# Output projections: the split of a row hung behind a product, one row ahead instead of two; the second pair's Gram masks 18 products sooner

## The chip, the core and the metric

The kernel runs on one core of a Trainium2 chip. The metric is the device time in microseconds (us) of one execution, as the median of several runs. The engines are called as the profile calls them: PE (TensorE, matrix products), DVE (VectorE), ACT (ScalarE), POOL (GpSimd) and SP (SyncE, which here issues most of the DMA transfers).

## What is computed

Two residual layers over 512 tokens of width 2048, in float32. Layer 0 is a gated differential attention with 8 heads, layer 1 a gated RWKV-7 time mixing with 32 heads of 64 channels; each ends with an output projection and a residual add. Cut to what matters:

```
for i in range(2):
    hn = rms_norm(x, norm_w[i])
    if i == 0:
        q, k, v, gate = split(hn @ w_in)            # 2048 -> 4 * 2048
        a = softmax(q1 k1^T) - lam * softmax(q2 k2^T)   # causal, per head
        y = rms_norm(a v) * silu(gate)
        out = y @ w_out                             # 2048 -> 2048
    else:
        p = hn @ w_in                               # 2048 -> 4 * 2048 + 2 * 96
        p = p + (shift(p) - p) * mu
        r, k, v, g, dw, da = split(p)
        for t in range(512):                        # per head, state S is 64 x 64
            S = S * w_t + (S a_t) b_t^T + v_t k_t^T
            y_t = S r_t
        out = (group_norm(y) * silu(g)) @ w_out     # 2048 -> 2048
    x = x + out
```

## The kernel before

Everything is computed with 128 partitions. A product in float32 precision is made of three products of halves: each operand is split into a rounded high half (hH, wh) and the rest (hL, wl), and `mm3` (line 118) issues high*high, high*low and low*high. A split is always one cast on ACT and one subtraction on DVE: lines 109 and 110 for weights (wh, wl from wraw), lines 474 and 475 for rows of activations (hH, hL from yr).

**Input projections** (`unit_chan`) give one block of 128 channels by 512 tokens in a bank pp: 16 blocks of the contracted dimension, three products each, so 48 products. Its argument `behind` is a list of pairs (number of products, function): when the count of products is reached, the function is called with the last product as `m` and issues its work there.

**Layer 1** handles two heads, a pair of 64 channels each, at a time: pair j has its own r, k, v and gate blocks. In `receptances(j)` the r block of pair j is projected, and work of pair j-1 hangs on its products: `mask_gram` masks the Gram products of pair j-1 with four affine selects on POOL (lines 1412 and 1414, two for each head). The hook stands at 45 for j = 1 and 2 and at 27 from j = 3 on. "Second pair" below is the pair masked in `receptances(2)`. Around it stand the scan's small products: gp (line 1367, the Gram product of AR with BK), sm (lines 1587, 1600, 1609), px (lines 1494 and 1509, the triangular solve), and ACT's copies of their results: rhs (line 1590), VS (1602), X (1497). AR (line 1351) is made on DVE of the shifted mix mixr (lines 1177 and 1178 hold the shift's two steps; mixE is the same for the gate). sHx (line 1145) is a cast for another product of the pair.

**Output projections** are made by `unit_tok`, 512 columns at a time: outputs are tokens by columns, in four banks, and weights come in steps of two rows of blocks (KG = 2), so 24 products for a step. Its callback `more` is called ahead of the triple products 0, 2 and 4 of a step with a row number n and the last product m. In the first column block of each layer the callback `all_rows` calls the object `feed` of class `Feed`, which loads the rows y of the mixer's output from DRAM (yd, yd2) and splits them with `split_row`. Its constructor loads six rows and splits four; then each call with n splits up to row n + 2 and loads up to row n + 8. In layer 0 some of these rows lie in a buffer Tt, the others in yr. The attention of the last head (exponentials p, lines 407 and 415; transposes pt, line 421) and in layer 1 the scan of the last pairs run among the products of that column block.

Two means set the order. `tc.issue_after(ins)` makes what is issued within it follow an instruction in a scheduler's list. `behind(g, ins, m)` gives one instruction an edge behind product m that orders it in its queue. Both only set the order of the queues: the instruction doesn't wait on the chip for the product.

Of the kernel before, what the change touches and what calls it, by code (L numbers as in the profile page):

```python
# [13 lines left out]
F32 = mybir.dt.float32  # L14
# [369 lines left out]
def attention(g, h, qkT, qkL, sq, vg, gap, rows=None, yT=None):  # L384
# [81 lines left out]
    if yT is not None:  # L466
        rows += [split_row(g, yT[:, c, :]) for c in range(2)]


def split_row(g, yr):  # L470
    nc = g.nc
    hh = g.hp.tile([P, T], F32R, name="hH", tag="hH")
    hl = g.hp.tile([P, T], F32R, name="hL", tag="hL")
    nc.scalar.copy(hh[:], yr)
    g.rowsplit = nc.vector.tensor_sub(hl[:], yr, hh[:].bitcast(F32)).ins
    return hh, hl


class Feed:
# [10 lines left out]
            self.raw.append(self.home(k))  # L490
            self.g.nc.sync.dma_start(out=self.raw[k], in_=self.src[k * P : (k + 1) * P, :])

    def split(self, upto, after=None):
        for k in range(len(self.rows), min(upto, self.n)):
            with self.g.tc.issue_after(after) if after else ExitStack():
                self.rows.append(split_row(self.g, self.raw[k]))

    def __call__(self, n):
        self.split(n + 2, self.g.split)
        self.load(n + 8)  # L500


# [25 lines left out]
class Seven:  # L528
# [70 lines left out]
    def behind(self, raw, h, i):  # L599

        if h + 1 < NH:
            landed = self.g.nc.gpsimd.tensor_copy(self.mark[:], raw[:, 0, 0:1])
            with self.g.tc.issue_after(landed.ins):
                self.prime(h + 1, True, GROUPS[i : i + 1])
        return raw
# [256 lines left out]
def layer0(g, aps):  # L862
    nc, tc = g.nc, g.tc
# [86 lines left out]
    with ExitStack() as cx:  # L950
# [15 lines left out]
        for h in range(1, NH):  # L966
# [3 lines left out]
        feed = Feed(g, g.yd, KT - 2, lambda k: g.work.tile([P, T], F32, name="yr", tag="t1", bufs=4)[:] if k & 4 else  # L970
                    Tt[:, k % 4])
        rows = feed.rows
        ch = Chain(g, attention(g, NH - 1, *before, 22, rows, Tt[:, 4:6]), 12)

        def all_rows(n, _):
            feed(n)
            if n >= KT - 1:
                ch.finish(g)

# [114 lines left out]
        def products(k, wt, s, m):  # L1094
            for c in range(2):
                wh, wl = [x[:, k % 4, c * RK : (c + 1) * RK] for x in wt]
                m = mm3(nc, pts[c][:RK, s], wh, wl, g.hH[k][:, s], g.hL[k][:, s],
                        k == 0 and s.start == 0, k == KT - 1, g, True)
            return m


        m, wts = g.m, []
        turns = [(k, half) for half in range(2) for k in range(0, KT // 2, 2)]
        for i, (k, half) in enumerate(turns):
# [6 lines left out]
            for kk in (k, k + 1):  # L1111
                m = products(kk, wts[kk // 4], slice(256 * half, 256 * half + 256), m)
        for k in range(KT // 2, KT):
# [3 lines left out]
            m = products(k, wts[k // 4], slice(0, T), m)  # L1117
        g.dwda = []
        for i in range(2):
            m = shift_mix(g, pts[i], RK, g.mut[:, i : i + 1], g.omut[:, i : i + 1], "t1", 4)  # L1120
# [51 lines left out]
@urgent  # L1172
def shift_mix(g, ps, rows, mu, omu, tag, bufs=2):

    nc, w = g.nc, g.work
    o_ = w.tile([P, T], F32, name="mix" + tag, tag=tag, bufs=bufs) if tag else g.ys.pop(0)
    nc.scalar.activation(o_[:rows, :], ps[:rows, :], AF.Copy, scale=omu)
    nc.vector.scalar_tensor_tensor(o_[:rows, 1:], ps[:rows, 0 : T - 1], mu, o_[:rows, 1:], ALU.mult, ALU.add)
    return o_
# [84 lines left out]
def mus(g, i, j):  # L1264
    n = i * 16 + j
    return g.mu[:, n : n + 1], g.omu[:, n : n + 1]
# [90 lines left out]
def gram(g, j, p):  # L1357

    nc, w, BK = g.nc, g.work, p.BK
    p.G = w.tile([P, NC_, 2, 2, C], F32, name="G1", tag="G1", bufs=2)  # L1360
    halves = []
    for c0, tag in ((0, "pb"), (4, "pc")):
        gp = [g.ps.tile([P, 512], F32, name="gp", tag=tag, bufs=2) for _ in range(2)]
        halves.append((c0, gp))
        for i in range(4):
            for h, r_ in ((0, slice(0, C)), (1, slice(C, P))):
                m = nc.tensor.matmul(gp[h][:, i * P : (i + 1) * P], BK[r_, c0 + i, :, :], p.AR[r_, c0 + i, :, :],  # L1367
                                     start=True, stop=True)
    p.LP = w.tile([P, NC_, HALF], F32, name="LP", tag="tmpl", bufs=1)
    with g.tc.high_priority(offset=AHEAD):  # L1370
        for c0, gp in halves:
            for h in range(2):
                for half in range(2):
                    q, o = h * C + half * HALF, half * HALF
                    nc.scalar.copy(p.LP[q : q + HALF, c0 : c0 + 4],
                                   gp[h][q : q + HALF].rearrange("p (u x) -> p u x", u=4)[:, :, o : o + HALF])

    def grams(c0, gp):
        for h in range(2):
            nc.scalar.copy(p.G[:, c0 : c0 + 4, :, h, :], gp[h][:].rearrange("p (u x t) -> p u x t", u=4, x=2))  # L1380

    g.soon.append(lambda: grams(*halves[0]))
    g.late.append(lambda: grams(*halves[1]))
    if not j:
        soon(g)
        soon(g, g.late)


def norms(g, j, p, m):

    nc, w = g.nc, g.work
    while g.later:
        g.later.pop(0)()
    ps = g.ps.tile([P, 512], F32, name="pt", tag="pb", bufs=2)
    with g.tc.issue_after(m.ins):
        sum_channels(g, ps[:2, :], g.ones[:, 0 : P : C], p.k2)
    ss = w.tile([2, T], F32, name="ssl", tag="thg", bufs=1)
    nc.scalar.copy(ss[:].rearrange("h (b c t) -> h c b t", b=2, c=NC_), ps[:2, :].rearrange("h (c b t) -> h c b t", c=NC_, b=2))
    nd = g.nd[j % 2]
    for half in range(2):  # L1400
        x = ss[:, half * NC_ * HALF : (half + 1) * NC_ * HALF]
        nc.gpsimd.dma_start(out=nd[:, half].rearrange("h r c t -> h r (c t)"),
                            in_=x[:, None].to_broadcast([2, NG, NC_ * HALF]))
    p.n2 = g.small.tile([P, HALF], F32, name="n2", tag="n2", bufs=1)
    nc.gpsimd.dma_start(out=p.n2[:], in_=nd.rearrange("h b r c t -> (h b r c) t"))


def mask_gram(g, p, h, m=None):

    nc = g.nc  # L1410
    for r_ in [slice(h * C, h * C + C)]:
        a = nc.gpsimd.affine_select(out=p.G[r_, :, 0, 1 - h, :], in_=p.G[r_, :, 0, 1 - h, :], compare_op=ALU.is_ge,
                                fill=0.0, base=-1, pattern=[[0, NC_], [1, C]], channel_multiplier=-1)
        b = nc.gpsimd.affine_select(out=p.G[r_, :, 1], in_=p.G[r_, :, 1], compare_op=ALU.is_ge, fill=0.0, base=0,
                                pattern=[[0, NC_], [0, 2], [1, C]], channel_multiplier=-1)
        behind(g, a, m)
        behind(g, b, m)
# [265 lines left out]
def layer1(g, aps):  # L1683
    nc, tc = g.nc, g.tc
    with ExitStack() as cx:
# [5 lines left out]
        pairs = []  # L1691

        def proj(i, j, **k):
            return unit_chan(g, aps["rw_w_in"][i, j], P, **k)[0]
# [10 lines left out]
        def receptances(j):  # L1705
            def piece(f, i, p):
                def follow(m):
                    with tc.high_priority(offset=SCAN), tc.issue_after(m.ins):
                        f(g, i, p)
                return follow  # L1710

            behind = [(39 if j == 1 else 39, lambda m: norms(g, j, pairs[j], m))]
            if j:
                behind += [(27 if j > 2 else 45, lambda m: [mask_gram(g, pairs[j - 1], h, m) for h in range(2)]),
                           (18 if j == 1 else 12, piece(t_first, j - 1, pairs[j - 1])),
                           (39 if j == 1 else 33, piece(t_second, j - 1, pairs[j - 1]))]
            return shift_mix(g, proj(0, j, behind=behind), P, *mus(g, 0, j), "r", 1)
# [3 lines left out]
        for j in range(D // P):  # L1721
# [16 lines left out]
            def behind(m, j=j, p=p):  # L1738
                if j > 1:
                    pairs[j - 2].chain.finish(g)  # L1740
                with tc.issue_after(m.ins):
                    gram(g, j, p)
                p.solve = Solve(g, t_solve(g, j, p))
# [23 lines left out]
        feed = Feed(g, g.yd2, KT - 2, lambda k: w.tile([P, T], F32, name="yr", bufs=1, tag=(  # L1767
            "r", "k", "th0", "th1", "l", "f", "xH", "xL")[k % 8])[:])
        rows = feed.rows

        def all_rows(n, m):
            feed(n)
            q = pairs[j - 1]
            if n >= 6 and not q.done:
                q.chain.finish(g)
                with tc.issue_after(m.ins):
                    finish_y(g, j - 1, q)
                    gated(g, j - 1, q, gts[0], True)
            if n >= 8 and len(rows) == KT - 2:
                rows.append(split_row(g, gts[0][:]))  # L1780
            if n >= KT and len(rows) < KT:
                p.chain.finish(g)
                finish_y(g, j, p)
                gated(g, j, p, gts[1], True)
                rows.append(split_row(g, gts[1][:]))
# [31 lines left out]
        for nm in ("11", "21", "22", "12"):  # L1817
            t, c = PLACES[nm]
            a = g.low.tile([P, 2, 512], F32, name="acc", tag="AR", bufs=3)
# [76 lines left out]
```

## Time and profile before

| | us |
|---|---|
| median of 3 runs | 2085.77 |
| lowest, highest run | 2085.66, 2087.77 |
| the profiled execution's own time | 2087.6 |
| its span in the profile | 2085.9 |
| PE busy in the span | 2066.0 |
| DVE, ACT, POOL busy | 1655.5, 1255.4, 392.3 |

The span is what the hardware profiler saw between the first and the last instruction of one execution; 1.7 us lie around it. In the profile's rows a time counts from the span's start, "L118" is line 118 of the kernel, and what stands in brackets is the idle time of the engine ahead of that instruction and what ended it. The granted clock (PEclk) is the share of its full rate that TensorE's clock was allowed, 1.00 at most. The layer 0 output projection starts at about 740 us, the Gram of the second pair lies near 1080 us, and layer 1's output projection starts at about 1895 us.

### The profile page before, as it was taken

How to read it: one execution, taken by the hardware profiler on the slowest of the kernel's cores; microseconds unless marked ns; L12 is line 12 of the kernel's file. 1: busy time of each engine (PE TensorE's matmuls, PEld its weight loads, DVE VectorE, ACT ScalarE, POOL GpSimd, SP SyncE). 2: the span in 40 equal slices, each digit the busy share in tenths (PEclk: the TensorE clock that was granted, in tenths of full speed). 3: DMA queues.
4: the chain of work that ended last, by engine and by line, in shares of the span. 5: the costliest groups of instructions: out<-in, count | busy, mean ns of one | idle time of the engine just before them, and what ended most of it. 6: DMA issues, size and time to landing. Idle time of an engine off the chain costs nothing. (4 is left out here: it accounts for less than half of the span.)

```text
span 2085.9 us, 35327 instructions
## 1 busy us (share of the span) xinstructions
PE 2066.0 (99%) x12008; PEld 1707.9 (82%) x12008; DVE 1655.5 (79%) x4353; ACT 1255.4 (60%) x3005; POOL 392.3 (19%) x716
## 2 busy tenths in 40 slices
PE   9999999999999999999999999999999999999999
PEld 7888888888888888887778888888888888877887
DVE  5978778787877886576878888888888888887745
ACT  5766666666666664455666666666666666665333
POOL 0111011111111000101223222323332223242001
PEclk9999999999999999999999999999999999999999
DMA  6577777778777766742222222222222222245665
GB/s 201 148 181 179 179 193 188 182 188 185 187 177 189 189 217 199 166 119 94 74 67 86 77 71 82 79 79 79 79 79 79 69 88 73 89 128 158 201 164 119
DMA packets 101780, 280.71 MB, mean 135 GB/s; under 512 B 12544, under 2 KB 29072, under 8 KB 101600
## 3 DMA queue, kind: packets, MB, share of 16 engines
q1 hardware_dynamic: 68064, 198.90, 29.4%
q0 software_dynamic: 19104, 63.55, 16.6%
q10 hardware_dynamic: 14432, 16.01, 2.2%
q8 instruction: 94, 1.54, 0.3%
q14 instruction: 86, 0.70, 0.1%
HBM read 262.42 MB, written 15.99 MB: 133 GB/s over the span
## 5 line engine op out<-in xcount | busy, mean ns | idle before, releaser
L118 PE MATMUL pp<-hH,wh 128*128 128x512 f32 x1024 | 416.8, 407 | 0.0
L118 PE MATMUL pp<-hL,wh 128*128 128x512 f32 x1024 | 412.0, 402 | 0.0
L118 PE MATMUL pp<-hH,wl 128*128 128x512 f32 x1024 | 411.9, 402 | 0.0
L109 ACT CAST wh<-wraw 128x512 fp32r<-128x512 f32 (+1 forms) x412 | 254.1, 618 | 223.1 <-PE pp L118 127.6
L118 PE MATMUL pp<-wh,hH 128*128 128x512 f32 x932 | 367.1, 394 | 0.0
L118 PE MATMUL pp<-wh,hL 128*128 128x512 f32 x932 | 366.9, 394 | 0.0
L110 DVE TENSOR_TENSOR wl<-wraw,wh 128x512 fp32r<-128x512 f32 (+1 forms) x412 | 292.8, 712 | 91.9 <-ACT wh L109 87.0
L118 PE MATMUL pp<-wl,hH 128*128 128x512 f32 x932 | 364.9, 391 | 0.0
L118 PEld LDWEIGHTS pp<-hH,wh 128*128 128x128 f32 x1024 | 192.9, 188 | 37.9 <-issue 1.5
L118 PEld LDWEIGHTS pp<-hH,wl 128*128 128x128 f32 x1024 | 193.2, 189 | 33.2
L118 PEld LDWEIGHTS pp<-hL,wh 128*128 128x128 f32 x1024 | 193.3, 189 | 31.3
L118 PEld LDWEIGHTS pp<-wh,hL 128*128 128x128 f32 x932 | 175.3, 188 | 35.9
L118 PEld LDWEIGHTS pp<-wl,hH 128*128 128x128 f32 x932 | 175.4, 188 | 35.2
L118 PEld LDWEIGHTS pp<-wh,hH 128*128 128x128 f32 x932 | 175.4, 188 | 34.1
L620 DVE TENSOR_TENSOR wl<-wraw,wh 128x512 fp32r<-128x512 f32 x224 | 152.4, 688 | 59.8 <-ACT wh L619 59.2
L619 ACT CAST wh<-wraw 128x512 fp32r<-128x512 f32 x224 | 138.3, 620 | 94.8 <-PE pp L118 66.0
L1595 POOL COPY SA<-VS 64x64 f32<-64x64 f32 x224 | 74.4, 332 | 520.8 <-DVE VS L1613 465.4
L118 PE MATMUL pp<-wh,S 128*128 128x512 f32 x504 | 162.1, 395 | 0.0
L1460 DVE SCALAR_TENSOR_TENSOR tmpl<-LT,n,Tm 128x60 f32<-128x60 f32 (+24 forms) x496 | 135.5, 273 | 13.3
L1463 DVE TENSOR_TENSOR Tm<-Tm,tmpl 128x60 f32<-128x60 f32 (+24 forms) x496 | 105.9, 214 | 13.1
L582 POOL DMA_DIRECT2D T<-in_da_w_in_dram x63 | 53.8, 858 | 326.5 <-DVE wl L620 313.0
L619 ACT CAST wh<-T 128x512 fp32r<-128x512 f32 x126 | 77.8, 618 | 52.2 <-PE pp L118 52.1
(375 smaller groups left out, 3943.9 us busy)
## 6 DMA issues: line engine op xcount, KB each, us to landing
wraw<-in_rw_w_in_dram SPq DMA_DIRECT2D x128, 512.0 KB, 3.6
wraw<-in_da_w_in_dram SPq DMA_DIRECT2D x127, 512.0 KB, 4.3
T<-in_da_w_in_dram POOLq DMA_DIRECT2D x63, 512.0 KB, 6.6
wraw<-in_da_w_out_dram SPq DMA_DIRECT2D x26, 512.0 KB, 4.4
wraw<-in_rw_w_out_dram SPq DMA_DIRECT2D x26, 512.0 KB, 4.1
T<-in_da_w_in_dram SPq DMA_DIRECT2D x21, 512.0 KB, 3.9
wraw<-in_da_w_in_dram POOLq DMA_DIRECT2D x21, 512.0 KB, 7.0
yr<-yd SPq DMA_DIRECT2D x20, 256.0 KB, 3.2
```

Of the source, the lines that this page charges most:

```text
L109: nc.scalar.copy(hi[:], raw[:, k : k + n])
L110: g.split = nc.vector.tensor_sub(lo[:], raw[:, k : k + n], hi[:].bitcast(F32)).ins
L118: m = nc.tensor.matmul(out, a, b, start=s, stop=e, skip_group_check=skip)
L582: self.g.nc.gpsimd.dma_start(out=raw, in_=src, accum_op=ALU.add)
L619: g.nc.scalar.copy(hi[:], raw[:, k])
L620: g.nc.vector.tensor_sub(lo[:], raw[:, k], hi[:].bitcast(F32))
L1460: st = nc.vector.scalar_tensor_tensor(tt, LT[:, i : i + 1, i + 1 :].to_broadcast([P, s, n]), n2[:, i : i + 1], Tm[:, 0:s, i : i + 1].to_br ...
L1463: nc.vector.tensor_add(Tm[:, 0:s, i + 1 :], Tm[:, 0:s, i + 1 :], tt)
L1595: nc.gpsimd.tensor_copy(p.SA[r_, c - 1, :], VS[r_, c, h, :])
```

## The change

The row split gets an argument m: with it, cast and subtraction hang behind product m by `behind`. `Feed` passes the product that TensorE is at, and each call with n splits up to row n + 1 instead of n + 2. Both layers' `all_rows` hand their m on. And the masks of pair 1 (in `receptances(2)`) hang at hook 27 instead of 45. The first four rows, which the constructor splits, have no m, as before. The lines of after stand two further down than those of before, from line 478 on.

```diff
--- before.py
+++ after.py
@@ -467,12 +467,15 @@
         rows += [split_row(g, yT[:, c, :]) for c in range(2)]
 
 
-def split_row(g, yr):
+def split_row(g, yr, m=None):
     nc = g.nc
     hh = g.hp.tile([P, T], F32R, name="hH", tag="hH")
     hl = g.hp.tile([P, T], F32R, name="hL", tag="hL")
-    nc.scalar.copy(hh[:], yr)
-    g.rowsplit = nc.vector.tensor_sub(hl[:], yr, hh[:].bitcast(F32)).ins
+    a = nc.scalar.copy(hh[:], yr)
+    b = nc.vector.tensor_sub(hl[:], yr, hh[:].bitcast(F32))
+    for x in (a, b) if m else ():
+        behind(g, x, m)
+    g.rowsplit = b.ins
     return hh, hl
 
 
@@ -490,13 +493,12 @@
             self.raw.append(self.home(k))
             self.g.nc.sync.dma_start(out=self.raw[k], in_=self.src[k * P : (k + 1) * P, :])
 
-    def split(self, upto, after=None):
+    def split(self, upto, m=None):
         for k in range(len(self.rows), min(upto, self.n)):
-            with self.g.tc.issue_after(after) if after else ExitStack():
-                self.rows.append(split_row(self.g, self.raw[k]))
-
-    def __call__(self, n):
-        self.split(n + 2, self.g.split)
+            self.rows.append(split_row(self.g, self.raw[k], m))
+
+    def __call__(self, n, m):
+        self.split(n + 1, m)
         self.load(n + 8)
 
 
@@ -972,8 +974,8 @@
         rows = feed.rows
         ch = Chain(g, attention(g, NH - 1, *before, 22, rows, Tt[:, 4:6]), 12)
 
-        def all_rows(n, _):
-            feed(n)
+        def all_rows(n, m):
+            feed(n, m)
             if n >= KT - 1:
                 ch.finish(g)
 
@@ -1711,7 +1713,7 @@
 
             behind = [(39 if j == 1 else 39, lambda m: norms(g, j, pairs[j], m))]
             if j:
-                behind += [(27 if j > 2 else 45, lambda m: [mask_gram(g, pairs[j - 1], h, m) for h in range(2)]),
+                behind += [(27 if j > 1 else 45, lambda m: [mask_gram(g, pairs[j - 1], h, m) for h in range(2)]),
                            (18 if j == 1 else 12, piece(t_first, j - 1, pairs[j - 1])),
                            (39 if j == 1 else 33, piece(t_second, j - 1, pairs[j - 1]))]
             return shift_mix(g, proj(0, j, behind=behind), P, *mus(g, 0, j), "r", 1)
@@ -1769,7 +1771,7 @@
         rows = feed.rows
 
         def all_rows(n, m):
-            feed(n)
+            feed(n, m)
             q = pairs[j - 1]
             if n >= 6 and not q.done:
                 q.chain.finish(g)
```

The order of instructions on the engines differs at three places. First POOL in the Gram of the second pair (SA, VS: the scan's state copies; Tm, nd, n: later steps of the same pair; G: the Gram products). Before:

```order
L1595 COPY SA<-VS 64x64 x2
L1584 MEMSET VS 64x64 x2
L1450 CAST Tm<-unit 128x256
L1402 DMA nd<-ssl 2x4x256 x2
L1412 AFFINE_SELECT G_11072<-G_11072 64x8x64
L1414 AFFINE_SELECT G_11072<-G_11072 64x8x128
L1412 AFFINE_SELECT G_11072<-G_11072 64x8x64
L1414 AFFINE_SELECT G_11072<-G_11072 64x8x128
L1405 DMA n_11739<-nd 128x32
```

After the change there stands:

```order
L1597 COPY SA<-VS 64x64 x2
L1586 MEMSET VS 64x64 x2
L1414 AFFINE_SELECT G_11072<-G_11072 64x8x64
L1416 AFFINE_SELECT G_11072<-G_11072 64x8x128
L1414 AFFINE_SELECT G_11072<-G_11072 64x8x64
L1416 AFFINE_SELECT G_11072<-G_11072 64x8x128
L1452 CAST Tm<-unit 128x256
L1404 DMA nd<-ssl 2x4x256 x2
L1407 DMA n_11743<-nd 128x32
```

The four selects have moved ahead of the cast Tm and the two DMAs of nd. At the same place on ACT, from the shift of r on, before:

```order
L1177 ACTIVATE mixr<-pp,omu 128x512
L109 CAST wh<-wraw 128x512
L1145 CAST sHx<-mixr 128x512
L1590 COPY rhs<-sm 64x64 x2
L1602 COPY VS<-sm 64x64 x2
L1375 COPY LP<-gp 32x128 x8
```

After the change there stands:

```order
L1179 ACTIVATE mixr<-pp,omu 128x512
L1592 COPY rhs<-sm 64x64 x2
L1604 COPY VS<-sm 64x64 x2
L109 CAST wh<-wraw 128x512
L1147 CAST sHx<-mixr 128x512
L1377 COPY LP<-gp 32x128 x8
```

The copies rhs and VS have moved ahead of a weight cast and the cast sHx.

At the start of layer 1's output projection, ACT before, from row casts of the constructor and of the first calls on:

```order
L474 CAST hH<-yr 128x512 x4
L1590 COPY rhs<-sm 64x64 x2
L474 CAST hH<-yr 128x512
L109 CAST wh<-wraw 128x512
L1602 COPY VS<-sm 64x64 x2
L474 CAST hH<-yr 128x512 x4
L109 CAST wh<-wraw 128x512
L474 CAST hH<-yr 128x512
L1658 ACTIVATE ysq<-yc 128x512
L474 CAST hH<-yr 128x512 x2
L1497 COPY X<-px 32x256 x2
L1500 COPY G_21150<-AR 64x8x64 x2
```

After the change there stands:

```order
L474 CAST hH<-yr 128x512 x2
L1592 COPY rhs<-sm 64x64 x2
L109 CAST wh<-wraw 128x512
L1604 COPY VS<-sm 64x64 x2
L1502 COPY G_21150<-AR 64x8x64
L1499 COPY X<-px 32x256 x2
L1502 COPY G_21150<-AR 64x8x64
L1660 ACTIVATE ysq<-yc 128x512
L109 CAST wh<-wraw 128x512 x2
L1179 ACTIVATE mixE<-pp,omu 128x512
```

Ten row casts that stood ahead of X stand further down; ysq and two weight casts now stand between X and mixE. PE at that place, with the tiles' numbers (pp_21708 and pp_21709 are two output banks of the projection, pt_21710 a third; the bank of pp_21709 held the gate's block that mixE reads), before:

```order
L1509 MATMUL px_21637<-W_21546,X_21636 32x32 x16
L118 MATMUL pp_21708<-wh_21718,hH_21696 128x512
L118 MATMUL pp_21708<-wl_21719,hH_21696 128x512
L118 MATMUL pp_21708<-wh_21718,hL_21697 128x512
L118 MATMUL pt_21710<-wh_21714,hH_21692 128x512
L118 MATMUL pt_21710<-wl_21715,hH_21692 128x512
L118 MATMUL pt_21710<-wh_21714,hL_21693 128x512
L118 MATMUL pt_21710<-wh_21718,hH_21696 128x512
L118 MATMUL pt_21710<-wl_21719,hH_21696 128x512
L118 MATMUL pp_21709<-wh_21714,hH_21692 128x512
```

After the change there stands:

```order
L1511 MATMUL px_21637<-W_21546,X_21636 32x32 x16
L118 MATMUL pp_21708<-wh_21718,hH_21696 128x512
L118 MATMUL pp_21708<-wl_21719,hH_21696 128x512
L118 MATMUL pp_21708<-wh_21718,hL_21697 128x512
L118 MATMUL pp_21709<-wh_21714,hH_21692 128x512
L118 MATMUL pp_21709<-wl_21715,hH_21692 128x512
L118 MATMUL pp_21709<-wh_21714,hL_21693 128x512
L118 MATMUL pp_21709<-wh_21718,hH_21696 128x512
L118 MATMUL pp_21709<-wl_21719,hH_21696 128x512
L1589 MATMUL sm_21764<-VS_21414,G1_21150 128x128
```

The products of pp_21709 now follow those of pp_21708 directly, ahead of those of pt_21710. On ACT in layer 0, at the start of the output projection, before:

```order
L474 CAST hH<-yr 128x512 x2
L474 CAST hH<-Tt 128x512 x4
L109 CAST wh<-wraw 128x512
L407 ACTIVATE p_8364,sm<-sc,nb,sq 128x128
L407 ACTIVATE p_8372,sm<-sc,nb,sq 128x128
L109 CAST wh<-wraw 128x512
L474 CAST hH<-yr 128x512 x2
L424 CAST at<-pt 128x128
```

After the change there stands:

```order
L474 CAST hH<-yr 128x512
L407 ACTIVATE p_8360,sm<-sc,nb,sq 128x128
L109 CAST wh<-wraw 128x512
L407 ACTIVATE p_8368,sm<-sc,nb,sq 128x128
L109 CAST wh<-wraw 128x512
L474 CAST hH<-yr 128x512
L424 CAST at<-pt 128x128
```

Five row casts have moved down from ahead of the first exponential, and a weight cast stands between the first two exponentials.

## The prediction, made before the changed kernel was run

> **What bounds the kernel now.** I read the page first (span and busy shares), then the waits of TensorE, then time windows around the three places where the order of instructions differs, then the timeline of those windows on every engine. Page lines:
>
> ```profile
> span 2085.9 us, 35327 instructions
> PE 2066.0 (99%) x12008; PEld 1707.9 (82%) x12008; DVE 1655.5 (79%) x4353; ACT 1255.4 (60%) x3005; POOL 392.3 (19%) x716
> ```
>
> TensorE is busy for 2066.0 of 2085.9 us: the product stream is the bound. The change takes no product away, so it can only win back idle time of TensorE (19.9 us in all) and stretches at a reduced clock. Of TensorE's waits, four stand where the change moves something (columns: total us, times, longest):
>
> ```profile
> PE sm L1600 <- ACT rhs L1590: 1.7, 1, 1.7
> PE px L1509 <- ACT X L1497: 1.4, 1, 1.4
> PE pt L421 <- DVE p L415: 0.7, 1, 0.7
> PE gp L1367 <- DVE AR L1351: 0.5, 1, 0.5
> ```
>
> The first and last lie in the Gram of the second pair, the second at the start of layer 1's output projection, the third at that of layer 0.
>
> **The masks.** The same stretch of work (69 PE instructions), from the Gram's first products on, in windows; first the second pair, then the third, whose masks already hang at hook 27. Columns: length, then busy of PE, PEld, DVE, ACT, POOL, then the granted clock and DMA:
>
> ```profile
> 1076.45:1089.07 12.62, 10.32 (x69) 8.08 (x67) 10.06 (x22) 5.07 (x13) 6.65 (x10) 1.00 0.19 61
> 1138.87:1148.31 9.44, 9.44 (x69) 7.81 (x67) 8.15 (x24) 6.26 (x16) 1.75 (x3) 1.00 0.35 112
> ```
>
> The second pair takes 12.62 us, TensorE busy for 10.32; the third 9.44, with TensorE never idle. POOL is busy 6.65 us there against 1.75. The timeline shows what POOL does:
>
> ```profile
> 1071.40 0.33 POOL L1584 MEMSET VS<- 64x64 f32 x2 [4.30 <-PE Y L1633]
> 1077.03 0.69 DVE L110 TENSOR_TENSOR wl<-wraw,wh 128x512 fp32r<-128x512 f32 x1
> 1078.43 0.17 DVE L68 SCALAR_TENSOR_TENSOR rs_t<-rs_t,var 128x8 f32<-128x8 f32 x1
> 1079.22 0.69 POOL L1412 TENSOR_SCALAR_AFFINE_SELECT G<-G 64x512 f32<-64x512 f32 x1
> 1079.38 1.66 DVE L68 SCALAR_TENSOR_TENSOR rs_t<-rs_t,var 128x8 f32<-128x8 f32 x1
> 1081.16 1.15 DVE L110 TENSOR_TENSOR wl<-wraw,wh 128x512 fp32r<-128x512 f32 x1
> 1081.73 1.60 POOL L1414 TENSOR_SCALAR_AFFINE_SELECT G<-G 64x1024 f32<-64x1024 f32 x1
> 1083.00 0.86 DVE L1351 TENSOR_TENSOR AR<-mixr,E 128x512 f32<-128x512 f32 x1
> 1083.92 0.49 PE L1367 MATMUL gp<-AR,BK 64*128 64x128 f32 x4 [0.47 <-DVE AR L1351]
> 1085.17 0.62 ACT L1145 CAST sHx<-mixr 128x512 fp32r<-128x512 f32 x1 [2.87 <-DVE mixr L1352]
> 1085.69 0.42 ACT L1590 COPY rhs<-sm 64x64 f32<-64x64 f32 x2
> 1086.16 0.44 PE L1600 MATMUL sm<-rhs,TT 128*128 128x64 f32 x2 [1.75 <-ACT rhs L1590]
> ```
>
> The masks run from 1079.22 to 1083.33. While they do, a DVE instruction of 0.17 us takes 1.66 and one of 0.69 takes 1.15: 1.95 us late in sum. So AR ends only at 1083.86 and gp waits 0.47. ACT's cast sHx, which has waited 2.87 us for DVE's mixr, stands ahead of the copy rhs, so L1600 waits 1.75. Together 2.22 us idle; the rest of 12.62 − 9.44 is products at wider spacing.
>
> After the change the four masks stand on POOL directly behind the memset of VS (row at 1071.40), ahead of Tm and nd; 4.1 us of masks end near 1076, before the stretch. On ACT, rhs and VS come ahead of wh's cast and sHx; on PE the order becomes word for word the third pair's. So the price is the third pair's: 12.62 − 9.44 = **3.2 us won**. Ends: nothing (masks slow DVE as much where they now are, which the next rival prices), and 3.2 (TensorE fully busy). I take 3.2. What moves behind the masks, Tm and the two DMAs of nd, starts up to 4.1 us later on POOL; the third pair has the masks first too, with no TensorE wait in its row.
>
> [...]
>
> **Rows split one ahead: start of layer 1's output projection.** Windows and timeline:
>
> ```profile
> 1904.00:1908.00 4.00, 4.00 (x26) 3.14 (x19) 2.16 (x5) 3.19 (x7) 0.00 (x0) 0.57 0.33 126
> ```
> ```profile
> 1894.95 0.68 DVE L475 TENSOR_TENSOR hL<-yr,hH 128x512 fp32r<-128x512 f32 x1
> 1898.92 0.62 DVE L1468 STREAM_TRANSPOSE T<-Tm 128x256 f32<-128x256 f32 x1
> 1899.59 0.69 PE L1494 MATMUL px<-T,G 32*32 32x32 f32 x32 [0.24 <-DVE T L1468]
> 1901.48 0.40 PE L118 MATMUL pp<-wl,hH 128*128 128x512 f32 x1
> 1901.71 0.40 PE L118 MATMUL pp<-wh,hL 128*128 128x512 f32 x1
> 1902.12 0.62 ACT L474 CAST hH<-yr 128x512 fp32r<-128x512 f32 x1 [1.72 <-DMA yr<-yd]
> 1902.75 0.74 ACT L1497 COPY X<-px 32x256 f32<-32x256 f32 x2
> 1903.54 0.69 PE L1509 MATMUL px<-W,X 32*32 32x32 f32 x32 [1.44 <-ACT X L1497]
> 1904.17 0.55 PE L118 MATMUL pp<-wh,hH 128*128 128x512 f32 x1
> 1904.79 0.69 ACT L1177 ACTIVATE mixE<-pp,omu 128x512 f32<-128x512 f32 x1
> 1905.51 0.75 DVE L1178 SCALAR_TENSOR_TENSOR mixE<-pp,prmin_rw_mu_dram,mixE 128x511 f32<-128x511 f32 x1 [1.34 <-ACT mixE L1177]
> 1907.48 6.46 SPq L76 DMA_DIRECT2D wraw<-in_rw_w_out_dram  x2
> 1907.91 0.39 PE L118 MATMUL pp<-wl,hH 128*128 128x512 f32 x1
> 1909.30 0.39 PE L118 MATMUL pt<-wh,hL 128*128 128x512 f32 x1
> 1909.83 0.41 PE L1600 MATMUL sm<-rhs,TT 128*128 128x64 f32 x2
> ```
>
> Before, twelve row casts stand on ACT ahead of X; the last waits 1.72 us for its row's DMA, X is copied only at 1902.75 and L1509 waits. From the last product to L1509 it is 1903.54 − 1901.71 = 1.83 us, where products follow each other at 0.23 (1901.48 to 1901.71): 1.6 lost. Right behind it the granted clock is 0.57 for four us: nine steps between products take 1907.91 − 1904.17 = 3.74 instead of 9 × 0.23 = 2.07, another 1.7.
>
> After the change X stands on ACT behind two row casts, rhs, a weight cast, VS and one G copy; ten row casts no longer stand ahead of it. px<-T (L1494) stands 12 products (2.8 us) earlier on PE, and T leaves DVE earlier, since subtracts of 0.68 (L475) no longer stand ahead of it; I take its wait unchanged at 0.24. So X is done before L1509: **1.6 won**. Ends: 0 and 1.6.
>
> The products of pp_21709, whose bank must first be read by mixE (L1177 on ACT, L1178 on DVE), now follow pp_21708's six directly instead of after five products of pt. TensorE would get there near 1903.4. mixE's last read ends at 1906.26 before, but ACT's start of it (1904.79) stood behind X; after, X stands some 4 us sooner, and ysq and two weight casts (0.61 each, row below) stand ahead of mixE instead. I estimate that its read ends at 1903.7, so a new wait of 0.3. Ends: 0, and 2.9 (mixE no earlier than before). Against it, L1600 a few products on started 0.53 after the product before it (1909.30 to 1909.83) where 0.23 is usual: 0.3 that I take to go, since rhs, too, has fewer casts ahead of it. Net nothing.
>
> If the gap goes, does the half clock go? The trace has the drop straight behind a gap of 1.44 us. [...]
>
> **Start of layer 0's output projection.**
>
> ```profile
> 747.27 2.18 ACT L474 CAST hH<-Tt 128x512 fp32r<-128x512 f32 x4
> 749.87 0.45 ACT L407 ACTIVATE p<-sc,nb,sq 128x128 f32<-128x128 f32 x1
> 750.75 0.61 ACT L109 CAST wh<-wraw 128x512 fp32r<-128x512 f32 x1
> 751.84 0.30 PE L421 MATMUL pt<-ident,p 128*128 128x128 f32 x1 [0.70 <-DVE p L415]
> ```
>
> Four row casts (2.18 us) stand ahead of the exponential; after, one. But a weight cast (0.61) now lies between the two exponentials. Ends 0 and 0.7 (the whole wait); I take the middle, **0.3 won**.
>
> **Splits elsewhere.** Each row still costs 0.62 on ACT and 0.68 on DVE, and hangs behind a product at least ten triples, 30 × 0.23 = 6.9 us, ahead of its first use: hidden by that lead. On SP the row loads of later rows move behind a weight load (wraw) that they stood ahead of; that weight load is issued at 1907.48 in any case, when its buffer is free, and the row loads are called for eight rows ahead of use. POOL's queue has nothing of the splits. I cost the splits at nothing, with 0 and rival D's price as ends: if the lead of 6.9 us were gone, each row would cost its cast and subtract on the path.
>
> **Sum.** The profiled execution took 2087.6 (span 2085.9): 3.2 + 1.6 + 1.7 + 0.3 = 6.8, giving 2080.8. It stands 1.8 above the median of 2085.77, about the price of the half clock, and one of three runs (2087.77) is like it. So I take the median to be without that drop: 3.2 + 1.6 + 0.3 = 5.1, giving **2080.7**; between the two, 2080.8.
>
> **Rivals.**
> A: the tail gives nothing, because mixE comes late and the new wait eats the 1.6 (it does from a wait of 1.6 on, mixE read by 1905.0; before it was 1906.26). Then 3.2 alone: 2082.6. Against: X no longer stands ahead of mixE.
> B: every run has the half clock, and the 1.8 is what profiling adds. Then 2085.77 − 6.8 = 2079.0. For: the only trace shows it; against: two of three runs lie 2 us under the third. [...]
> C: the masks carry their slowing along: whatever DVE does at 1072 to 1076 is late by the same 1.95 us and AR is late as before; only rhs's new place on ACT is won. Then 1.75 + 1.6 + 0.3 = 3.6, so 2082.1. Against: the third pair's full row.
> D, on the other side: splits behind products come too late, and TensorE waits for them row by row. It decides from the point where cast and subtract come more than the 6.9 us lead behind their product. Then up to 0.62 + 0.68 = 1.3 for each of some ten rows: 13 − 5.1, so 2093.7. Against: ACT is busy 60%, DVE 79%.
>
> **How the numbers follow.** Forecast 0.48, A 0.17, B 0.2, C 0.11, D 0.04. About 0.2% (4.2 us, to 2081.6) is what a measurement of this kernel can tell from no change. B counts as faster, with nearly all of the forecast, whose own spread is 2079.9 to 2082: 0.2 + 0.46 = 0.66. A, C and the rest are the same: 0.3; D slower: 0.04. The range leaves out D and the far ends: from 2078.7 (B with a wait or two more gone) to 2083.2 (A without layer 0's 0.3, and some new wait).
>
> **What would show it.** Masks: the stretch of the second pair near 9.4 us, no wait of L1367 or L1600 there, L68 at 0.17. Tail: no wait at L1509, clock 1.00 behind it, a wait of mixE under 0.5. Layer 0: L421's wait near 0.4. Wrong would make it: a new wait of products for hH or hL (D), or for mixE above 1.6 (A), or a half clock that comes back behind another gap.

## The result, and the profile after

The changed kernel takes 2080.86 us (median of 7 runs, 2079.82 to 2082.15); the kernel before 2087.47 (median of 7, 2085.61 to 2089.64; the three runs of the table above are among them). The ratio is 0.9971 with a 95% interval of 0.9959 to 0.9982: by the ratio 6.0 us won, 3.8 to 8.6; by the medians 6.6. The predicted 2080.8 was met to 0.1 us, with a base and a gain that were both some 1.6 us too small by the medians (below). The profiled execution took 2079.82 us. Its page begins:

```profile
span 2078.1 us, 35336 instructions
PE 2062.8 (99%) x12008; PEld 1705.7 (82%) x12008; DVE 1652.8 (80%) x4353; ACT 1255.9 (60%) x3005; POOL 393.9 (19%) x716
```

The span is 7.8 us shorter: TensorE's busy time fell by 3.2 us, its idle time by 4.6 (19.9 to 15.3). The same number of products takes less busy time: at the start of layer 1's output projection 18.13 us instead of 20.00, with the clock at 1.00 instead of 0.92, and in the second pair's Gram 9.40 instead of 10.32, with the clock at 1.00 both times (windows below). Of the four waits shown before, those for rhs, X and AR are gone from TensorE's list of waits; the fourth is smaller:

```profile
PE pt L421 <- DVE p L415: 0.2, 1, 0.2
```

**The Gram of the second pair.** Windows again, from the products of sHx and sLx to the first product behind the Gram:

```profile
1075.85:1085.25 9.40, 9.40 (x68) 7.77 (x66) 8.14 (x23) 5.74 (x15) 2.62 (x7) 1.00 0.31 99
```

9.40 us instead of 12.62, with TensorE never idle. The timeline shows POOL's masks, and DVE and ACT behind them:

```profile
1071.18 0.65 POOL L1414 TENSOR_SCALAR_AFFINE_SELECT G<-G 64x512 f32<-64x512 f32 x1
1071.31 1.06 DVE L1148 TENSOR_TENSOR sLx<-k,sHx 128x512 fp32r<-128x512 f32 x1 [0.62 <-ACT sHx L1147]
1074.48 1.16 POOL L1416 TENSOR_SCALAR_AFFINE_SELECT G<-G 64x1024 f32<-64x1024 f32 x1
1079.12 0.17 DVE L68 SCALAR_TENSOR_TENSOR rs_t<-rs_t,var 128x8 f32<-128x8 f32 x1
1079.48 0.42 ACT L1592 COPY rhs<-sm 64x64 f32<-64x64 f32 x2
1080.79 0.69 DVE L1353 TENSOR_TENSOR AR<-mixr,E 128x512 f32<-128x512 f32 x1
1083.43 0.69 DVE L1148 TENSOR_TENSOR sLx<-mixr,sHx 128x512 fp32r<-128x512 f32 x1
```

The masks run from 1071.18 to 1075.64. They still slow what DVE does beside them in part (sLx takes 1.06 there and 0.69 later, while wl at 1073.32 takes 0.68), but nothing that TensorE waits for in this stretch. L68 takes 0.17, AR ends at 1081.48, and rhs is copied ahead of the pair's sHx.

**The start of layer 1's output projection.** Windows between the same two points of the program, the products Y of the last scan step ahead of it and the transposes of yc behind it; first the kernel before, then after:

```profile
1893.92:1915.74 21.82, 20.00 (x193) 15.18 (x193) 16.73 (x47) 12.49 (x28) 4.62 (x10) 0.92 0.63 199
```
```profile
1889.96:1908.26 18.30, 18.13 (x193) 14.20 (x193) 13.35 (x42) 10.31 (x24) 4.50 (x9) 1.00 0.71 226
```

3.52 us less, with 193 PE instructions in both, and the clock at 1.00. From the timeline after:

```profile
1894.13 0.74 ACT L1499 COPY X<-px 32x256 f32<-32x256 f32 x2
1897.95 0.69 PE L1511 MATMUL px<-W,X 32*32 32x32 f32 x32
1898.78 0.74 DVE L1180 SCALAR_TENSOR_TENSOR mixE<-pp,prmin_rw_mu_dram,mixE 128x511 f32<-128x511 f32 x1
1899.14 0.39 PE L118 MATMUL pp<-wh,hL 128*128 128x512 f32 x1
1899.58 0.50 PE L118 MATMUL pp<-wh,hH 128*128 128x512 f32 x1
```

X is there 3 us ahead of the product that needs it. px<-T starts 0.51 behind the product ahead of it (1892.78 and 1892.27; before, 0.63). mixE's read ends at 1899.52, and the product that needs its bank starts 0.44 behind the one before it instead of 0.23: a wait of 0.2. It isn't new. In the first profile of before it can't be seen, since all products stand 0.43 apart there, at a granted clock of 0.50; the second one (next section) has the same product 0.42 behind the one ahead of it:

```profile
1905.39 0.39 PE L118 MATMUL pt<-wl,hH 128*128 128x512 f32 x1
1905.81 0.50 PE L118 MATMUL pp<-wh,hH 128*128 128x512 f32 x1
```

**Layer 0.** The wait at L421 is smaller and a new one stands further on:

```profile
750.77 0.30 PE L421 MATMUL pt<-ident,p 128*128 128x128 f32 x1 [0.19 <-DVE p L415]
...
778.52 0.41 PE L445 MATMUL yt<-ident,y 128*128 128x128 f32 x2 [0.28 <-DVE y L440]
```

### The profile page after: what moved, and what is told of

The parts are those of the page before. It is cut to its first block, busy times and chain, and to the rows that moved or that the text cites. A ratio compares the mean times of both kernels' runs of the same rounds, so it can differ in the third digit from the quotient of the medians.

```text
span 2078.1 us, 35336 instructions
## 1 busy us (share of the span) xinstructions
PE 2062.8 (99%) x12008; PEld 1705.7 (82%) x12008; DVE 1652.8 (80%) x4353; ACT 1255.9 (60%) x3005; POOL 393.9 (19%) x716
```

## The experiments

Theory 1 is the prediction's: the masks' place costs 3.2 us, X's wait 1.6, and a half clock (a granted clock of 0.50) behind X's wait 1.7 in some executions. The rivals are its B (that half clock in every execution) and C (the masks carry their slowing along). Each run's ratio is to the kernel before on the same chip, with its 95% interval.

**The kernel before, once more.**

> The kernel before, once more, for a second profile of it and for the spread between equal kernels. Both theories: ratio 1.000 within 0.001; the stretch of the second pair's Gram 12.6 us; the wait for X at the start of layer 1's output projection 1.4 us. Theory 1 (the half clock behind that wait is of some runs only): a profiled execution near 2085.7 us shows a granted clock of 1.00 at 1900 to 1910 us and no products 0.43 us apart, one near 2087.6 shows the drop again. Rival B (it belongs to the wait, in every run): the drop of some 1.7 us is there in this profile, whatever its time.

Measured: ratio 0.9998 (0.9990 to 1.0007); 2087.52 us against 2087.14 for 32 runs of before. So the 2085.77 from which I started was low: two of its three runs lie in the lower part of a spread from 2084.3 to 2090.0. This profile, of an execution of 2085.39 us, in the same two stretches:

```profile
1076.11:1088.73 12.62, 10.32 (x69) 8.07 (x67) 10.06 (x22) 5.07 (x13) 6.65 (x10) 1.00 0.19 62
...
1893.63:1913.98 20.35, 18.74 (x193) 13.96 (x193) 16.74 (x47) 12.50 (x28) 4.61 (x10) 1.00 0.69 216
```

The Gram is the same to 0.01 us. At the output projection the wait for X is there (1.2 us), but no half clock: 20.35 against 21.82. Rival B is out.

**Only the masks.**

```diff
-                behind += [(27 if j > 2 else 45, lambda m: [mask_gram(...)
+                behind += [(27 if j > 1 else 45, lambda m: [mask_gram(...)
```

> Before, with the second pair's masks at hook 27 and nothing else. My theory: the stretch of its Gram 9.4 us instead of 12.6, and 3.2 us off the time (ratio 0.9985). Rival C (the masks carry their slowing along): only rhs's place on ACT is won, 1.75 us (ratio 0.9992). The start of layer 1's output projection as before: 1.4 us of wait for X; by theory 1 its half clock may be there or not, by rival B it is there.

Measured: ratio 0.9975 (0.9966 to 0.9984), 5.2 us won, more than the 3.2 of my theory and far from rival C's 1.75. The stretch as expected:

```profile
1078.14:1087.54 9.40, 9.40 (x68) 7.78 (x66) 8.15 (x23) 5.74 (x15) 2.62 (x7) 1.00 0.31 99
```

Rival C falls. That the time gains 2 us more than the profiles' 3.2 is taken up below.

**Only the splits.** The changed kernel with 45 for the second pair's masks.

```diff
-                behind += [(27 if j > 1 else 45, ...
+                behind += [(27 if j > 2 else 45, ...
```

> Before, with the rows' splits behind products, one ahead, in both layers, and the masks at 45 as before. My theory: 1.6 us (the wait for X) and at most 0.3 in layer 0 off a run without the half clock, and 1.7 more off one with it: 1.9 to 3.6, ratio 0.9983 to 0.9991; the stretch of the Gram stays at 12.6. Rival B: 3.6 us in every run. Rival A (a later wait gives it back): 0.3 at most.

Measured: ratio 0.9998 (0.9988 to 1.0007). The output projection gains in full (18.32 us between the two points of the program), and yet the time hardly moves: the 1.9 to 3.6 us that I expected didn't come. The profile shows where they go:

```profile
1078.05:1091.53 13.48, 11.17 (x69) 8.83 (x67) 10.06 (x22) 5.35 (x14) 6.66 (x10) 0.93 0.17 56
```

The Gram's stretch has a mean clock of 0.93: a half clock behind the Gram's waits this time, which costs 1.6 us up to where the clock is full again (15.22 us from the stretch's start to the fifth product behind the Gram, 13.66 in the first profile of before).

**The masks twice.** Which part of the Gram's loss is POOL beside DVE, and which the order on ACT? In the masks-only kernel the first pair's Gram, long masked, is masked again at the old hook.

```diff
+                if j == 2:
+                    behind.append((45, lambda m: [mask_gram(g, pairs[0], h, m) for h in range(2)]))
```

> The masks-only kernel with four more selects on POOL at the old place, hook 45, on the first pair's Gram, which they leave as it is. The order on PE, ACT and DVE is that of the masks-only kernel word for word; only POOL has more to do where the masks stood. [...] If the order on ACT alone is the cause: nothing comes back (ratio 0.9985, stretch 9.4). My theory has both: AR late and gp waits 0.5 to 1, but rhs no longer waits behind sHx, so some 0.5 to 1 us come back (stretch 9.9 to 10.4).

Measured: ratio 0.9986 (0.9977 to 0.9995), 2084.52 us against 2082.23 for the masks alone: 2.3 come back. The window of the stretch, then rows of POOL, DVE and PE:

```profile
1077.05:1088.01 10.96, 9.47 (x68) 7.77 (x66) 10.36 (x21) 5.07 (x13) 5.53 (x8) 1.00 0.28 86
```
```profile
1080.36 0.68 POOL L1412 TENSOR_SCALAR_AFFINE_SELECT G<-G 64x512 f32<-64x512 f32 x1
1080.51 1.66 DVE L67 TENSOR_TENSOR rs_t<-rs_i 128x8 f32<-128x8 f32 x1
1082.20 0.66 DVE L68 SCALAR_TENSOR_TENSOR rs_t<-rs_t,var 128x8 f32<-128x8 f32 x1
1085.28 0.69 DVE L1351 TENSOR_TENSOR AR<-mixr,E 128x512 f32<-128x512 f32 x1
1086.03 2.06 PE L1367 MATMUL gp<-AR,BK 64*128 64x128 f32 x32 [1.49 <-DVE AR L1351]
```

With no other queue changed, small DVE instructions beside POOL's selects are slow again (1.66 and 0.66 us in the rows, 0.16 to 0.17 for the same lines just ahead of the selects), AR is late, and gp waits 1.49. That costs 1.56 us in this stretch (10.96 against 9.40), where I had given it 0.5 to 1: POOL beside DVE alone holds TensorE up. What its share is of the 3.22 us that the stretch loses in the kernel before, this run doesn't say. AR starts 8.23 us into the stretch here, 6.55 in the kernel before and 4.93 with the masks alone, so the selects struck harder here. The wait for rhs doesn't return, since rhs stays ahead of sHx on ACT. In the kernel before, sHx itself waited 2.87 us for DVE's mixr, which the masks had made late; how much of the 1.75 there is the order on ACT and how much the slowed DVE, no run separates.

**What makes the split work: the edge, or one row less?** Two ahead with the edge; one ahead without.

```diff
-        self.split(n + 1, m)
+        self.split(n + 2, m)      # e5
+        self.split(n + 1)         # e6
```

> The changed kernel with rows split two ahead as before, but still behind the product that TensorE is at. PE's order stays word for word that of the changed kernel; on ACT one or two row casts stand some places sooner. My theory (the edge behind the product is what counts, not the number of rows): the same time as the changed kernel, ratio to before 0.997, no wait for X above 0.3 us. Rival (one row less is what counts): X waits again, some 1.6 us more, ratio 0.9978.

Measured: ratio 0.9970 (0.9959 to 0.9982), 2081.05 us: the changed kernel's time.

```profile
1890.80:1909.09 18.29, 18.13 (x193) 14.19 (x193) 13.76 (x43) 10.84 (x25) 4.49 (x9) 1.00 0.75 238
```

> The changed kernel with rows split one ahead, but with no product behind which they hang. On ACT the row casts pile up ahead of X nearly as before. My theory: the wait for X at the start of layer 1's output projection is back with 0.6 to 1.6 us, and the time is that of the masks-only kernel, ratio to before 0.9975 to 0.998. Rival (one row less is what counts): no wait for X, ratio 0.997.

Measured: ratio 0.9985 (0.9976 to 0.9994), 2083.71 us: 3 us behind the changed kernel, and no better than the masks alone (2082.23). From the profile, the window and the rows:

```profile
1891.30:1914.03 22.73, 21.09 (x193) 16.41 (x193) 17.71 (x51) 12.63 (x28) 7.21 (x10) 0.85 0.74 243
```
```profile
1897.13 0.62 ACT L474 CAST hH<-yr 128x512 fp32r<-128x512 f32 x1 [1.19 <-DMA yr<-yd]
1900.55 0.61 DVE L1470 STREAM_TRANSPOSE T<-Tm 128x256 f32<-128x256 f32 x1
1901.21 0.69 PE L1496 MATMUL px<-T,G 32*32 32x32 f32 x32 [1.53 <-DVE rs_i L64]
```

Row casts that wait for their DMA pile up ahead of ACT's and DVE's work for the scan. The wait now stands at L1496, for T (T and the rs_i that the row names end at the same time, 1901.16), not at X as I expected, and a half clock follows. The order on PE differs here too: px<-T stands behind products of pp and pt that follow it in the changed kernel. So what the edge does, it does through the order of all the queues. The edge behind the product makes the gain; one row or two makes no difference that shows.

**All masks at 27.**

```diff
-                behind += [(27 if j > 1 else 45, ...
+                behind += [(27, ...
```

> The changed kernel with the first pair's masks at hook 27 too. Only POOL's order changes: the four selects move ahead of the two DMAs of nd, the four copies TT and the cast Tm. At that place TensorE waits 1.22 us for VS (1030.00 in the changed kernel's profile), and DVE has instructions of 1.65 and 2.25 us beside POOL's masks. If the masks there are what makes VS late, up to 1.2 us are won (ratio to the changed kernel 0.9994); if the chain of the first pair itself is, nothing changes (within 0.5 us), and if TT behind the masks holds the scan's first step, up to 3 us are lost.

Measured: 2082.42 us, ratio 0.9974 (0.9964 to 0.9984), 1.8 us above the changed kernel's 2080.62 on the same chip. One line of the waits and one of POOL tell why:

```profile
PE pt L1275 <- DVE sLx L1148: 1.9, 1, 1.9
```
```profile
988.41 1.60 POOL L1416 TENSOR_SCALAR_AFFINE_SELECT G<-G 64x1024 f32<-64x1024 f32 x1
```

The first pair's masks now run at 986 to 990 us. In the changed kernel's profile only the first of the four stands there, at 984.69, the others from 1020.10 on. From the first select to sLx on DVE it is 28.78 us (985.94 to 1014.72), in the changed kernel 27.12 (984.69 to 1011.81): sLx comes 1.66 us later, and the product for sLx waits 1.9 us instead of 0.5. No expectation of mine had this wait, and the one for VS that I wanted to win stays, at 1.3. Sooner isn't better in itself.

**The changed kernel once more.**

> The changed kernel once more, beside the others on one chip, for a second profile. Both theories: ratio to before 0.997. Theory 1 (a half clock of some 1.6 us falls behind gaps of over one us in some executions): its runs spread over some 2.5 us against 5.7 of before, since the two largest gaps inside the layers are gone; the profile has no half clock at 1900 to 1910 or at 1076 to 1092. Rival (the spread comes from elsewhere): the runs spread as widely as those of before.

Measured: ratio 0.9966 (0.9954 to 0.9979), 2080.62 us (2080.56 to 2081.41 in 5 runs); Gram 9.40 and no half clock at either place. All 12 runs of the changed kernel lie within 2.3 us, against 5.7 of before.

**More profiles, for the half clock.** Two of the splits alone, two of before.

> The splits-only kernel again, for a second profile. Theory 1 (a half clock is of some executions, by chance, behind a gap): about as often as not none behind the Gram's wait, and then a time some 1.6 us below 2086.9, near 2085; one with it near 2087. Theory 2 (with the first gap of layer 1's end gone, the half clock behind the Gram's wait is there in every execution): again 0.7 or less at 1088 to 1092 us, and no run below 2085.5.

> As the run ahead: a third profile of the splits-only kernel. Theory 1: with or without a half clock behind the Gram's wait. Theory 2: with it.

> The kernel before, a third profile. Theory 1: a half clock behind the Gram's wait (1088 to 1092 us) or behind X's (1904 to 1908 us) or at neither place, each worth some 1.6 us, and a time of 2085.4 with none, 2087 with one, 2088.6 with both. Rival B: the one behind X's wait in any case.

> The kernel before, a fourth profile, as the run ahead: the time follows the number of half clocks, 1.6 us for each, from 2085.4 with none.

Measured: the splits alone at 0.9990 (0.9981 to 1.0000), profiles of 2087.19 and 2085.92 us; before at 2087.72 and 2090.48. The Gram's window in the four profiles, in this order:

```profile
1077.08:1091.52 14.44, 12.23 (x69) 9.70 (x67) 10.07 (x22) 5.34 (x14) 6.66 (x10) 0.85 0.16 54
```
```profile
1076.00:1090.65 14.65, 12.44 (x69) 9.90 (x67) 10.06 (x22) 5.33 (x14) 6.66 (x10) 0.82 0.16 54
```
```profile
1075.75:1090.39 14.64, 12.43 (x68) 9.89 (x66) 10.07 (x22) 5.35 (x14) 6.66 (x10) 0.83 0.15 54
```
```profile
1078.40:1093.13 14.73, 12.43 (x68) 9.90 (x66) 10.14 (x22) 5.38 (x14) 6.75 (x10) 0.82 0.16 54
```

All four have a half clock there; DVE and POOL have the same work as in 12.62. Small windows show how long one lasts; columns here are the length, PE busy, the granted clock and DMA. First the third profile of before, then the first of the splits alone:

```profile
1085.20:1085.60 0.40, 0.13 (x1) 0.89 0.00 0
1085.60:1086.00 0.40, 0.40 (x2) 0.50 0.00 0
...
1091.60:1092.00 0.40, 0.40 (x3) 0.50 0.00 0
1092.00:1092.40 0.40, 0.40 (x3) 0.58 0.00 0
```
```profile
1089.60:1090.00 0.40, 0.40 (x10) 0.61 0.00 0
1090.00:1090.40 0.40, 0.40 (x8) 0.50 0.00 0
...
1092.40:1092.80 0.40, 0.40 (x2) 0.50 0.00 0
1092.80:1093.20 0.40, 0.40 (x2) 0.62 0.00 0
```

With the edges worked out inside the outer windows (a mean of 0.61 is 0.78 of the window at half), the first lasts from 1085.51 to 1092.34, 6.83 us, the second from 1089.69 to 1093.10, 3.41. All the profiles together, in us; "Gram" and "projection" are the lengths of the two stretches:

| profile | its time | Gram | half clock behind it | projection | half clock in it |
|---|---|---|---|---|---|
| before | 2087.6 | 12.62 | none | 21.82 | 3.4 |
| before, second | 2085.39 | 12.62 | none | 20.35 | none |
| before, third | 2087.72 | 14.64 | 6.8 | 20.18 | none |
| before, fourth | 2090.48 | 14.73 | 6.8 | 20.34 | none |
| splits only | 2086.96 | 13.48 | 3.4 | 18.32 | none |
| splits only, second | 2087.19 | 14.44 | 6.8 | 18.29 | none |
| splits only, third | 2085.92 | 14.65 | 6.8 | 18.30 | none |
| masks only | 2083.56 | 9.40 | none | 19.72 | none |
| masks twice | 2085.71 | 10.96 | none | 20.74 | none |
| one ahead, free | 2085.41 | 9.40 | none | 22.73 | 6.8 |
| after | 2079.82 | 9.40 | none | 18.30 | none |
| after, second | 2080.73 | 9.40 | none | 18.33 | none |
| two ahead, behind | 2080.61 | 9.40 | none | 18.29 | none |

So the half clock is of some executions, as theory 1 had it, but it mostly sits at the other wait: behind the Gram's in 5 of 7 profiles that have the full wait there, behind X's in 1 of 6. Theory 1's price of 1.6 us is that of one length of 3.4 us; two cost 2.7 to 2.9. The fourth profile of before, with three lengths in all (one at 924 us), took 2090.48 us, where 1.6 for each from 2085.4 on gives 2090.2.

Each run's mean granted clock is on record too. In the profiled executions it is 1.000 without a half clock, 0.999 with one length of 3.4 us, 0.998 with two and 0.997 with three, wherever they lie. Theory 2 of these runs (in the splits-only kernel the half clock is always there) fits all three profiles, but 4 of that kernel's 22 runs have 1.000, at 2084.75 to 2085.58 us: theory 2 is out. Of the 77 runs of before that have a clock on record:

| mean granted clock | runs | median, us |
|---|---|---|
| 1.000 | 14 | 2085.5 |
| 0.999 | 27 | 2087.0 |
| 0.998 | 25 | 2088.6 |
| 0.997 | 11 | 2089.8 |

Of the 12 runs of the changed kernel 11 have 1.000, with a median of 2080.6. Among runs without a half clock the change is thus worth 4.8 us; the rest of the measured 6 to 7 goes with half clocks that come less often.

How many lengths follow can be compared with where the edges lie. In the fourth profile of before one stretch of half clock starts at 923.93 and one at 1087.77 us, 163.84 apart, which is 48.00 times 3.413. In the first profile of before the stretch behind X's wait lasts from 1904.47 to 1907.88, and the half clock behind TensorE's last product, where it slows nothing (the changed kernel has it too, from 2077.65), starts at 2085.37, 177.49 after that end, 52.00 times 3.413. So in these two executions the edges lie on a fixed grid of 3.413 us. From execution to execution it lies differently: in the five profiles with a half clock behind the Gram's waits, that starts 9.37 to 11.64 us behind the start of the stretch. So I estimate that the same waits fall into one interval of the grid or are cut in two. TensorE's idle time in the 3.413 us just ahead of the half clock was 2.21 and 1.87 us in the third and fourth profile of before, and 1.58, 2.21 and 1.89 in the three of the splits alone: 3.4 us behind the 1.58, 6.8 behind the others. In the first profile of before, counted back from 1904.47, an edge of the grid falls at 1085.26, into the wait for rhs; the two parts hold 1.31 and 0.99 us of idle time, and no half clock follows. The 1.58 of the splits alone drew 3.4 us, and 1.53 in the kernel with one row ahead and no edge drew 6.8, so idle time isn't all that counts; what else does stays open.

## Why the prediction was right, and what in it was not

- **Masks, 3.2 us.** Right in mechanism and, without a half clock, to the tenth: 12.62 to 9.40, as the third pair's stretch had said. But where the waits of 0.5 and 1.7 us draw a half clock of 6.8 us behind them, the place costs some 6 us (the same products lie 5.95 to 6.14 us later, against the changed kernel, in the four profiles that have it, and 3.26 in those without). The term that was mis-sized is this one: in the median about 5, the 5.2 of the masks alone; among runs without a half clock the masks alone are worth 3.7.
- **X's wait, 1.6 us.** Without a half clock the stretch takes 20.18 to 20.35 us before and 18.30 after: 1.9 to 2.05. Against the second profile of before, px<-W,X starts 1.28 us sooner behind the product ahead of it (1.60, now 0.32), px<-T 0.11, and the next products for rhs and VS 0.30 and 0.14. So X's own term was 1.3, not 1.6. The 0.3 for rhs came as forecast, but mixE's wait of 0.2, which I had set against it as new, was there before.
- **The half clock behind X's wait, 1.7.** Its size was right (1.5: 21.82 against 20.35), its place was chance. I read one profile as the rule of this gap, took the drop to go with it, and took the difference of 1.8 us between that execution and the median as its price. The step that failed is "I take the median to be without that drop": the median of many runs of before is 2087.1 to 2088.5, not 2085.77, 63 of 77 runs have a half clock somewhere by their mean granted clock, and three of the four profiles have one at one of the two places, two of them behind the Gram's waits.
- **Layer 0, 0.3.** Nothing. L421's wait varies in before by itself (none, 0.34, 0.70 and 0.95 us in its four profiles); after, it is 0.19 with a new 0.28 or 0.29 at L445 in both profiles. From the transposes at 736 us to those at 785 us the changed kernel takes 48.9 us, before 48.4 to 49.2.
- **Sum.** 5.1 us off 2085.77 and, as measured, 6.0 to 7.1 off 2087.5 to 2087.8 end at the same time. The sum of the waits isn't luck: the changed kernel is an execution without any half clock among its products less the two waits, 2085.39 − 3.2 − 2.0 = 2080.2. That the median of three runs was such an execution is luck: 14 of 77 runs are.
- **Rivals.** A is out (mixE's wait is 0.2), C, which prices the lower end of the masks' term, is out as far as TensorE goes (sLx takes 1.06 us beside the masks where they now are, 0.69 later, but TensorE is never idle from 1070.80 to 1085.25), D is out (no product waits for hH or hL of a row). Of B the sum of 6.8 was near, its place wrong.

## What to carry to other kernels

When POOL works beside DVE, ask whom DVE is working for at that moment: four selects cost nothing at one place and about 2 us at two others (1.8 and 2.3). Work that runs ahead (casts of rows) belongs behind a product that TensorE is at, not in front of the scan's short chain: in the kernel before, a cast that waited 1.72 us for its row's DMA stood ahead of X on ACT, and TensorE waited 1.44 us for X; whether one row or two ran ahead made no difference. And before a difference of 2 us in 2000 is read, profile the same kernel more than once: two profiles of the kernel before were 5.1 us apart. The mean granted clock of each run tells which runs can be compared (for before, medians of 2085.5 us at 1.000 and 2089.8 at 0.997).

## What the runs showed of the hardware that I had not expected

- Among the products the half clock came in lengths of 3.41 or 6.83 us, and the same waits in the same program drew none, one or two such lengths. In the two profiles that show two stretches of it apart, the edges lie 48.00 and 52.00 times 3.413 us apart. TensorE's idle time in the 3.413 us ahead of it was 1.44 us at X's wait (first profile of before), 1.53 at T's (one ahead, free) and 1.58 to 2.21 at the Gram's (five profiles); on the grid of the first profile of before the longest idle time in an interval with no half clock behind it was 1.33 us (918.01 to 921.43). The half clock stood also at 924 us, between the layers, in 2 of the 13 profiles of the table (the masks alone and the fourth of before), for 3.4 us each.
- A DVE instruction of 128 x 8 elements took 0.17 us alone and up to 1.66 beside POOL's selects, which take 0.65 to 1.60. Those of 128 x 512 in the rows above went from 0.69 to between 0.86 and 1.15, and wl at 1020.15 in the changed kernel to 1.65.
- With two waits of TensorE gone, of 2.2 and 1.4 us, the runs spread over 2.3 us (12 of them) against 5.7 (32 of before): most of the spread came from half clocks, by the medians of the table 4.3 us between none and three lengths.
